# Projecting into transposed columns: which operand of the matmul stays, and which streams

## The chip, the cores and the metric

The kernel runs on one core of a Trainium2 chip. The metric is device time in microseconds (us) of one execution. The kernel before took 1302.33 us (median of three runs, 1302.3 to 1302.5).

## The reference

A sequence of 256 positions with 1024 features goes through two layers. Each layer is a half-step gated feed-forward network (FFN), a mixer, and a second half-step FFN; every part sits between a norm before and a norm after. The mixer of layer 0 is a dilated window attention with three groups of 16 heads, that of layer 1 a retention. Cut to what the change touches:

```
def rms_norm(x, g):
    y = xf * lax.rsqrt(jnp.mean(xf * xf, axis=-1, keepdims=True) + NORM_EPS)
    return y * g
def swiglu(h, w_gate, w_up, w_down):
    return (jax.nn.silu(h @ w_gate) * (h @ w_up)) @ w_down
...
    h = swiglu(rms_norm(x, g[0]), w_gate, w_up, w_down)      # 1024 -> 2816 -> 1024
    x = x + 0.5 * rms_norm(h, g[1])
    proj = (h @ w_in).reshape(B, S, 3 groups, q/k/v, 16 heads, 64)
    s = einsum('nbqhd,nbkhd->nbhqk', q, k) * 64 ** -0.5 + bias
...
```

Everything is float32. The projections of the norm before are linear, so the norm's gain can be folded into the weight's rows and its factor 1/rms, one number per position, can be applied behind the matmul.

## The kernel before, in words

**Positions** are held as two tiles of 128 (t = 0, 1). `xh` and `xl` hold the transposed input x of a part, features on the partitions, split into two float32r numbers whose sum is x; `pre_half` (L217) makes them with TensorE transposes.

**Weights** stream in once. `Stream` loads a block of 512 KB or 1 MB ("raw", two buffers), and `split` (L92) turns a piece of 256 rows by 512 columns (or 128 by 1024) into `whi` on ScalarE (L109, L115) and `wlo`, the rest, on VectorE (L110, L116). Six such pieces are in a ring, so splitting runs ahead of TensorE and is let on when TensorE gives a piece back (`done`, L135).

**A product** of x and w is three float32r matmuls, xh·whi, xh·wlo and xl·whi (`mm3`, L184 to L186). In all of them the x tile of 128 positions is the operand that stays in the array (LDWEIGHTS) and 512 weight columns stream. The result has positions on the partitions and columns along the row. A *unit* (`unit`, L319) is 512 output columns: 4 pieces of 2 row blocks, for 2 position tiles, 3 matmuls each, which is 48 matmuls of 512 columns into two PSUM banks.

**An FFN** (`ffn`, L363) has 11 units: gate and up columns in turn for five chunks of 512 (u = 0 to 9), and one unit of the last 256 gate and 256 up columns (u = 10). Behind a gate unit ScalarE takes Silu of the bank, scaled by the norm's factor `rstd` as one number per partition (L387); behind an up unit VectorE multiplies bank, factor and gate to h (L393). The down projection needs h with its columns on the partitions. So `h_store` (L336) transposes it, four blocks to a bank by TensorE (L342), ScalarE copies the bank to `hhf` (L349) and VectorE takes the rest `hlf` (L350). These transposes are put off to the second piece of the next unit (`pend`, `flush`). `down` (L414) then runs 22 row blocks and ends in `post` (L250): the norm behind the part, with its square sums, a small Newton iteration, and the sum with the residual.

**Attention** (`attn`, L532) has 18 units: q and k of three groups, then v of three groups, twice (8 heads each). q and k are wanted with the 64 numbers of a head on the partitions. After each q or k unit ScalarE copies the bank with the factor (L569), TensorE transposes eight blocks (L626), and VectorE copies them out (L628 for q, reversed; L630 for k).

**The order.** Each engine runs its instructions in one fixed order, which the language's scheduler makes from the program's order and from the buffers; inside `manual_schedule` it is the written one. Loads of weights and the small copies between layouts all go through SyncE's queue (SP). There are six PSUM banks for accumulators and two for transposes.

Of the kernel before, what the change touches and what calls it, by code (L numbers as in the profile page):

```python
# [14 lines left out]
P = 128  # L15
# [3 lines left out]
EPS = 1e-6  # L19
NK = D // P  # L20
# [120 lines left out]
class Trunk:  # L141
# [18 lines left out]
    def setup(self):  # L160
        nc, sb = self.nc, self.sb

        self.gcol = sb.tile([P, 96], F32, name="gcol")

        self.x = [sb.tile([P, D], F32, tag=f"x{t}", name=f"x{t}") for t in range(2)]
        xr = self.x_in[0].rearrange("(i r) d -> r i d", r=4)
        gr = sb.tile([96, P], F32, tag="sg", bufs=2, name="gr")
        nc.sync.dma_start(gr, self.norm_gains.rearrange("l n (k p) -> (l n k) p", p=P))
        for t in range(2):
            for rr in range(2):  # L170
                nc.sync.dma_start(self.x[t][rr * 64 : rr * 64 + 64, :], xr[2 * t + rr])
            self.ws.dma(halves=t == 0)
        self.ident = sb.tile([P, P], F32, name="ident")
        make_identity(nc, self.ident)
        warm = self.acc("warm")
# [29 lines left out]
    def rsqrt(self, ss, name, mean, out=None):  # L205

        nc, n = self.nc, ss.shape[1]
        t = self.sm.tile([P, 4 * n], F32, tag="nwt%d" % n, bufs=3, name=f"nw_{name}")
        v, y, u, r = (t[:, i * n : i * n + n] for i in range(4))
        nc.vector.tensor_scalar(out=v, in0=ss, scalar1=mean, scalar2=EPS, op0=ALU.mult, op1=ALU.add)  # L210
        self.newton(v, y, u)
        r = r if out is None else out
        nc.vector.tensor_scalar(out=r, in0=y, scalar1=1.0 / NEWTON, scalar2=None, op0=ALU.mult)
        return r


# [30 lines left out]
        self.pre_sums(name, 1, ss)  # L247
        self.rsqrt(ss, f"pre_{name}", 1.0 / D, self.rstd)

    def post(self, t, banks, gb, name):  # L250

        nc, sb = self.nc, self.sb
        w = self.sm.tile([P, 5], F32, tag="pn", bufs=3, name=f"pn_{name}_{t}")
        junk = sb.tile([P, 512], F32, tag="tmpb", bufs=1, name=f"psq_{name}_{t}")
        yg = sb.tile([P, D], F32, tag="tmpa", bufs=1, name=f"yg_{name}_{t}")
        for h in range(2):
            s = slice(h * 512, h * 512 + 512)
            nc.scalar.activation(junk, banks[h], AF.Square, scale=2.0**-5, accum_out=w[:, h : h + 1])
            nc.vector.tensor_tensor(out=yg[:, s], in0=banks[h], in1=gb[:, s], op=ALU.mult)
        v, y, u = (w[:, i : i + 1] for i in (2, 3, 4))  # L260
        nc.vector.scalar_tensor_tensor(out=v, in0=w[:, 0:1], scalar=EPS, in1=w[:, 1:2], op0=ALU.add, op1=ALU.add)
# [57 lines left out]
    def unit(self, pieces, accs, cols=(0, P), quota=2):  # L319
        for j, pc in enumerate(pieces):  # L320
# [3 lines left out]
                self.flush()  # L324
            self.work(quota)

    def flush(self):
        while self.pend:
            self.pend.pop(0)()
# [21 lines left out]

    def to_natural(self):

        self.xn = [self.sb.tile([P, D], F32, tag=f"E{t}", name=f"xn{t}") for t in range(2)]
        for T in range(2):
            for rr in range(2):
                for t in range(2):
                    self.nc.sync.dma_start(
                        self.xn[t].rearrange("(i r) d -> r i d", r=4)[2 * T + rr],
                        self.x[T][rr * 64 + 32 * t : rr * 64 + 32 * t + 32, :],  # L360
                    )

    def ffn(self, plan, nxt):  # L363
        nc, sb = self.nc, self.sb
        l, n = plan["l"], plan["n"]
        name = f"f{l}{n}"
        natural = l == 0 and n % 6 == 4
        for u, pieces in enumerate(plan["units"]):
            c = u // 2
            accs = {t: self.acc(f"ac_{name}_{u}_{t}") for t in range(2)}  # L370
            if u == 0:
                self.first_unit(pieces, accs)
                gb = self.load_gpost(l, n % 6 + 1, 0.5)
                self.hh = sb.tile([P, DFF // P, 2 * P], F32R, tag="A", name=f"hh{name}")
                self.hl = sb.tile([P, DFF // P, 2 * P], F32R, tag="B", name=f"hl{name}")
                if natural:
                    self.to_natural()
                if plan["tables"] is not None:
                    self.ret_tables(plan["tables"])
            else:  # L380
                self.unit(pieces, accs)
            w = 512 if u < 10 else 256
            if u % 2 == 0:
                sg = []
                for t in range(2):
                    g = sb.tile([P, 512], F32, tag="sg", bufs=2, name=f"sg_{name}{c}{t}")
                    nc.scalar.activation(g[:, :w], accs[t][:, :w], AF.Silu, scale=self.rstd[:, t : t + 1])  # L387
                    sg.append(g)
            if u % 2 == 1 or u == 10:
                for t in range(2):  # L390
                    h = sb.tile([P, 512], F32, tag="h", bufs=2, name=f"h_{name}{c}{t}")
                    up = accs[t][:, :512] if u < 10 else accs[t][:, 256:512]
                    nc.vector.scalar_tensor_tensor(out=h[:, :w], in0=up, scalar=self.rstd[:, t : t + 1], in1=sg[t][:, :w], op0=ALU.mult, op1=ALU.mult)  # L393
                    self.pend.append(lambda c=c, t=t, h=h, w=w: self.h_store(c, t, h, w, natural))
        hh, hl = self.hh, self.hl
        if natural:
            self.x = self.xn
        self.down(plan["down"], DFF // P, lambda k, t: (hh[:, k, t * P : (t + 1) * P], hl[:, k, t * P : (t + 1) * P]),
                  {3: self.flush}, gb, name, nxt)

    def first_unit(self, pieces, accs):

# [8 lines left out]

    TAIL = 5

    def down(self, pieces, rows, hT, hooks, gb, name, nxt, ntail=TAIL):  # L414


        ws = self.ws
        acc = [[self.acc(f"d_{name}_{t}{h}") for h in range(2)] for t in range(2)]
# [22 lines left out]
        self.post(0, acc[0], gb, name)  # L441
        for k in tail[:-2]:
            row(k, 1)
        for h in range(2):
# [5 lines left out]
                    self.pre_half(0, hh, name)  # L450
        if nxt is None:
            self.nc.sync.dma_start(self.out[0, :P, :], self.x[0])
            self.post(1, acc[1], gb, name)
# [5 lines left out]
        self.post(1, acc[1], gb, name)  # L459
        for h in range(2):  # L460
            self.pre_half(1, h, name)
        for k in tail[:2]:
# [69 lines left out]
    def attn(self, plan, nxt):  # L532
        nc, sb = self.nc, self.sb
        l = plan["l"]
        gb = self.load_gpost(l, 3, 1.0)
        OT = []
        rq = ru = None
        tasks_o1 = None
        for u, (o, kind, g, pieces) in enumerate(plan["units"]):
            accs = {t: self.acc(f"at_{u}_{t}") for t in range(2)}  # L540
            if kind == "q" and g == 0:
                bias, loads = self.bias_load(o)
            if u == 0:
                self.first_unit(pieces, accs)
                rq = self.sm.tile([P, 2], F32, tag="rq", name="rq")
# [3 lines left out]
                tr = self.trb("rut")  # L549
# [3 lines left out]
                nc.vector.tensor_copy(ru[0:64, :], tr[0:64, 0:2])  # L553
                nc.vector.tensor_copy(ru[64:128, 0:1], tr[64:128, 1:2])
                nc.vector.tensor_copy(ru[64:128, 1:2], tr[64:128, 0:1])
            else:
                for _ in range(2):
                    if loads:
                        loads.pop(0)()
                self.unit(pieces, accs, cols=(64, 192) if (kind == "v" and g == 2) else (0, P))  # L560
            if kind != "v":
                if kind == "q":
                    if g == 0:
                        qk = []
                    qk.append(sb.tile([P, 2, 4, 256], F32, tag=f"C{g}", name=f"qk{o}{g}"))
                w = 0 if kind == "q" else 1
                for t in range(2):
# [394 lines left out]
```

## Time and profile before

| | before |
|---|---|
| median of the runs | 1302.33 us |
| the profiled execution | 1302.6 us, its span 1300.5 us |
| TensorE (PE) matmuls busy | 1283.4 us, 99% of the span, 6326 records |
| TensorE weight loads (PEld) busy | 1052.9 us, 81% |
| VectorE (DVE) busy | 864.5 us, 66% |
| ScalarE (ACT) busy | 711.9 us, 55% |
| read from memory | 232.21 MB, 179 GB/s |
| granted TensorE clock, mean | 0.995 |

A row of the timeline gives the start of an instruction in us, its recorded length, engine, line, what it writes and reads, and shapes. Consecutive matmuls overlap in the records: each is listed at about 0.39 us, while the next one starts after little more than half of that. The time that a matmul costs is therefore read from start to start. In a row of the grouped view the number behind the bar is the group's busy time, then the mean recorded length in ns. An engine transpose and a float32 matmul (not float32r) are records of the same kind; the float32 matmul of the program stands as two records.

### The profile page before, as it was taken

Reading aid. Unit: us, or ns where it says so; the run is one execution under the profiler, and the core shown is the slowest. Engines: PE = TensorE matmul, PEld = TensorE weight load, DVE = VectorE, ACT = ScalarE, POOL = GpSimd, SP = SyncE. Lnnn points to the kernel's source line nnn. Section 1 sums busy time; section 2 is a strip of 40 time slices with the busy share of each in tenths; the row PEclk is TensorE's granted clock in tenths of the full one; section 3 lists DMA queues with packets and bytes.
Section 4 is the critical chain, followed back from the end, with each engine's and each line's share of the span. In section 5 each row is a group of like instructions: output and inputs, shape, how many; then the busy total and the mean of one; then the engine's idle time right before and its main releaser. Section 6 shows DMA issues by size and latency. Waiting matters only on the chain.

```text
span 1300.5 us, 16640 instructions
## 1 busy us (share of the span) xinstructions
PE 1283.4 (99%) x6326; PEld 1052.9 (81%) x6326; DVE 864.5 (66%) x1541; ACT 711.9 (55%) x1103; POOL 19.8 (2%) x16
## 2 busy tenths in 40 slices
PE   8999999999999999999999999999999999999997
PEld 6878887877887778888888888877888888888886
DVE  5765557678467768765477565489787775766544
ACT  4655444566555658764456554455555545565532
POOL 1000001000000000000000000000000000000000
PEclk8999999999999999999999999999999999999999
DMA  6755566754664346655547555645454555565551
GB/s 216 237 186 183 176 219 184 208 196 150 191 194 162 130 151 219 205 172 186 194 152 231 184 194 183 206 145 166 159 178 150 173 179 195 158 206 182 183 194 65
DMA packets 129692, 235.45 MB, mean 181 GB/s; under 512 B 25020, under 2 KB 41900, under 8 KB 129613
## 3 DMA queue, kind: packets, MB, share of 16 engines
q1 hardware_dynamic: 129468, 234.14, 55.6%
q8 instruction: 49, 0.80, 0.2%
q10 hardware_dynamic: 144, 0.26, 0.1%
q14 instruction: 31, 0.25, 0.1%
HBM read 232.21 MB, written 1.12 MB: 179 GB/s over the span
## 4 chain that ended last, share of the span: by engine, by line
PE 90%; DVE 4%; DMA 3%; ACT 2%; issue 1%; SPq 0%; DVEq 0%; ACTq 0%
PE ac_f L184 12%; PE ac_f L185 12%; PE ac_f L186 12%; PE d_f L184 6%; PE d_f L186 6%; PE d_f L185 6%; PE at L184 5%; PE at L186 5%; PE at L185 5%; PE rt L186 3%; PE rt L185 3%; PE rt L184 3%; DMA raw<-in_ret_w_in_dram 2%; PE htr L342 1%; DVE wlo L116 1%; PE ptt L678 1%
## 5 line engine op out<-in xcount | busy, mean ns | idle before, releaser
L116 DVE SCALAR_TENSOR_TENSOR wlo<-raw,gcol,whi 128x512 fp32r<-128x512 f32 x596 | 417.9, 749 | 184.3 <-ACT whi L115 183.5
L115 ACT ACTIVATE whi<-raw,gcol 128x512 fp32r<-128x512 f32 x596 | 393.7, 715 | 263.3 <-PE ac_f L186 88.4
L110 DVE TENSOR_TENSOR wlo<-raw,whi 128x1024 fp32r<-128x1024 f32 x112 | 137.3, 1226 | 137.9 <-ACT whi L109 137.6
L109 ACT ACTIVATE whi<-raw 128x1024 fp32r<-128x1024 f32 x112 | 118.8, 1061 | 165.3 <-PE d_f L186 101.2
L184 PE MATMUL d_f<-whi,hhf 128*128 128x512 f32 x352 | 137.6, 391 | 0.0
L186 PE MATMUL d_f<-whi,hlf 128*128 128x512 f32 x352 | 137.0, 389 | 0.0
L185 PE MATMUL d_f<-wlo,hhf 128*128 128x512 f32 x352 | 137.0, 389 | 0.0
L184 PE MATMUL at<-whi,xh_f 128*128 128x512 f32 x276 | 110.7, 401 | 0.0
L186 PE MATMUL at<-whi,xl_f 128*128 128x512 f32 x276 | 107.8, 391 | 0.0
L185 PE MATMUL at<-wlo,xh_f 128*128 128x512 f32 x276 | 107.4, 389 | 0.0
L185 PE MATMUL rt<-wlo,xh_f 128*128 128x512 f32 x244 | 95.8, 392 | 0.0
L184 PE MATMUL rt<-whi,xh_f 128*128 128x512 f32 x244 | 95.7, 392 | 0.0
L186 PE MATMUL rt<-whi,xl_f 128*128 128x512 f32 x244 | 95.1, 390 | 0.0
L186 PEld LDWEIGHTS d_f<-whi,hlf 128*128 128x128 f32 x352 | 66.1, 188 | 13.9
L184 PEld LDWEIGHTS d_f<-whi,hhf 128*128 128x128 f32 x352 | 66.1, 188 | 13.5
L185 PEld LDWEIGHTS d_f<-wlo,hhf 128*128 128x128 f32 x352 | 66.1, 188 | 13.4
L184 PE MATMUL ac_f<-whi,xh_in 128*128 128x512 f32 x176 | 70.4, 400 | 1.9 <-ACT whi L115 1.7
L185 PE MATMUL ac_f<-wlo,xh_in 128*128 128x512 f32 x176 | 69.9, 397 | 0.0
L186 PE MATMUL ac_f<-whi,xl_in 128*128 128x512 f32 x176 | 69.8, 396 | 0.0
L184 PE MATMUL ac_f<-whi,xh_at 128*128 128x512 f32 x168 | 65.9, 393 | 0.2 <-ACT xh_at L226 0.2
L186 PE MATMUL ac_f<-whi,xl_at 128*128 128x512 f32 x168 | 65.6, 390 | 0.0
L185 PE MATMUL ac_f<-wlo,xh_at 128*128 128x512 f32 x168 | 65.4, 389 | 0.0
(290 smaller groups left out, 2159.1 us busy)
## 6 DMA issues: line engine op xcount, KB each, us to landing
raw<-in_ffn_w_down_dram SPq DMA_DIRECT2D x44, 1024.0 KB, 4.9
raw<-in_ffn_w_up_dram SPq DMA_DIRECT2D x40, 1024.0 KB, 5.0
raw<-in_ffn_w_gate_dram SPq DMA_DIRECT2D x39, 1024.0 KB, 5.1
raw<-in_attn_w_in_dram SPq DMA_DIRECT2D x36, 1024.0 KB, 5.1
raw<-in_ret_w_in_dram SPq DMA_DIRECT2D x24, 1024.0 KB, 5.4
raw<-in_ret_w_in_dram SPq DMA_DIRECT2D x16, 512.0 KB, 4.6
raw<-in_ret_w_out_dram SPq DMA_DIRECT2D x8, 1024.0 KB, 4.9
raw<-in_ffn_w_gate_dram SPq DMA_DIRECT2D x10, 512.0 KB, 3.8
```

The lines of the kernel that those rows point to most:

```text
L109: nc.scalar.activation(hi, raw, AF.Copy)
L110: nc.vector.tensor_tensor(out=lo, in0=raw, in1=hi.bitcast(F32), op=ALU.subtract)
L115: nc.scalar.activation(hi[:, s], raw[:, s], AF.Copy, scale=gc)
L116: nc.vector.scalar_tensor_tensor(out=lo[:, s], in0=raw[:, s], scalar=gc, in1=hi[:, s].bitcast(F32), op0=ALU.mult, op1=ALU.subtract,)
L184: mm(out, xh, wh, start=start, stop=False)
L185: mm(out, xh, wl, start=False, stop=False)
L186: mm(out, xl, wh, start=False, stop=stop)
L342: nc.tensor.transpose(tr[:, k * P : (k + 1) * P], h[:, k * P : (k + 1) * P], self.ident)
L678: self.nc.tensor.transpose(tr[:, c * P : (c + 1) * P], pr[:, c * P : (c + 1) * P], self.ident)
```

## The change: what it does

For the FFN units u = 2 to 10 and for all q and k units but the first, the operands change places: 128 weight columns stay in the array and all 256 positions stream (`unit_t`). The result comes out with columns on the partitions, which is what the down projection and the scores want, so the transposes behind these units go. Each old matmul of 512 streamed columns becomes two of 256.

The norm's factor is then no longer one number per partition. `rows` makes it a row that is the same on all partitions (a diagonal matrix times ones, one float32 matmul), and VectorE multiplies the gate's bank, or the q or k bank, by it. The up half gets no factor in any unit: h stays too large by 1/rstd, one number per position, which the norm behind the part cancels, if its eps is multiplied by the variance of the norm before. `rsqrt` writes this scaled eps, `post` adds it in place of the constant, and where the positions are put into another order (`to_natural`) eight small copies move it too. The units u = 0 and 1 and the first q unit keep the old layout.

```
+    def unit_t(self, pieces, accs, quota=2):
+        mm = self.nc.tensor.matmul
+        for j, pc in enumerate(pieces):
+            hi, lo = self.ws.get(pc)
+            for kk in range(2):
+                k = 2 * j + kk
+                xh, xl = (z[:, k, 0 : 2 * P] for z in (self.xh, self.xl))
+                for c in range(4):
+                    b, a = divmod(c, 2)
+                    out = accs[b][:, a * 256 : a * 256 + 256]
+                    s = slice(kk * 512 + c * P, kk * 512 + c * P + P)
+                    mm(out, hi[:, s], xh, start=k == 0 and a == 0, stop=False, ...)
+                    mm(out, hi[:, s], xl, start=False, stop=False, ...)
+                    mm(out, lo[:, s], xh, start=False, stop=k == NK - 1, ...)
+            self.ws.done(pc)
+            if j == 1:
+                self.flush()
+            self.work(quota)
+    def ffn_t(self, u, pieces, name, natural, st):
+        accs = [self.acc(f"ac_{name}_{u}_{b}") for b in range(2)]
+        self.unit_t(pieces, accs)
+        if u % 2 == 0:
+            r = st["r"].unsqueeze(1).to_broadcast([P, 2, 2 * P])
+            for b in range(2 if u < 10 else 1):
+                g = sb.tile([P, 512], F32, tag="sg", bufs=2, ...)
+                nc.vector.tensor_tensor(out=g..., in0=accs[b]..., in1=r, op=ALU.mult)
+                nc.scalar.activation(g, g, AF.Silu)
...
+        for b, up in enumerate(accs if u < 10 else accs[1:]):
+            nc.vector.tensor_tensor(out=h, in0=up, in1=st["sg"][b], op=ALU.mult)
...
+            nc.scalar.activation(hi, hv, AF.Copy)
+            nc.vector.tensor_tensor(out=lo, in0=hv, in1=hi.bitcast(F32), op=ALU.subtract)
+    def rows(self, cols, name):
+        for t in range(2):
+            nc.vector.tensor_scalar(out=d[:, t, :], in0=self.ident, scalar1=cols[:, t : t + 1], ...)
+        nc.tensor.matmul(tr[:, : 2 * P], self.ones, d, start=True, stop=True)
+        nc.vector.tensor_copy(r, tr[:, : 2 * P])
 in rsqrt:
+            nc.vector.tensor_scalar(out=self.eps, in0=v, scalar1=EPS, scalar2=None, op0=ALU.mult)
 in post:
-        nc.vector.scalar_tensor_tensor(out=v, in0=w[:, 0:1], scalar=EPS, in1=w[:, 1:2], ...)
+        nc.vector.scalar_tensor_tensor(out=v, in0=w[:, 0:1], scalar=EPS if eps is None else eps[:, t : t + 1], in1=w[:, 1:2], ...)
 in to_natural, eight times:
+                    self.nc.sync.dma_start(self.eps[:, t : t + 1]...[2 * T + rr], eps[rr * 64 + 32 * t : rr * 64 + 32 * t + 32, T : T + 1])
 in ffn:
+            if u > 1:
+                self.ffn_t(u, pieces, name, natural, st)
+                continue
...
+                self.pend.append(lambda: st.update(r=self.rows(self.rstd, "f")))
...
-                    nc.vector.scalar_tensor_tensor(out=h[:, :w], in0=up, scalar=self.rstd[:, t : t + 1], in1=sg[t][:, :w], ...)
+                    nc.vector.tensor_tensor(out=h, in0=accs[t], in1=sg[t], op=ALU.mult)
 in attn:
+                self.pend.append(lambda rq=rq: scales.update(q=self.rows(rq, "q"), k=self.rows(self.rstd, "k")))
...
+                if kind == "v":
+                    self.unit(...)
+                else:
+                    self.unit_t(pieces, accs)
...
+                if u:
+                    for b in range(2):
+                        dst = qk[g][:, w, 2 * b : 2 * b + 2, :].rearrange("p a (r i) -> p a r i", r=4)
...
+                        nc.vector.tensor_tensor(out=dst, in0=src, in1=sc..., op=ALU.mult)
```

How the instructions stand before and after is shown at three places. The first is TensorE in unit 4 of the first FFN, at the end of its second piece; `ac_f_4_0` and `ac_f_4_1` are the unit's two banks, `htr` a bank for transposes. Before:

```order
L186 MATMUL ac_f_4_1_547<-whi_452,xl_in 128x512
L342 MATMUL htr_591<-ident,h_f_542 128x128 x4
L342 MATMUL htr_598<-ident,h_f_544 128x128 x4
L184 MATMUL ac_f_4_0_546<-whi_478,xh_in 128x512
L185 MATMUL ac_f_4_0_546<-wlo_479,xh_in 128x512
L186 MATMUL ac_f_4_0_546<-whi_478,xl_in 128x512
```

After:

```order
L377 MATMUL ac_f_4_1_660<-xh_in,wlo_512 128x256
L375 MATMUL ac_f_4_0_659<-xh_in,whi_551 128x256
L376 MATMUL ac_f_4_0_659<-xl_in,whi_551 128x256
L377 MATMUL ac_f_4_0_659<-xh_in,wlo_552 128x256
L375 MATMUL ac_f_4_1_660<-xh_in,whi_551 128x256
```

The eight transposes are gone, and every matmul streams 256 instead of 512. In the whole program 2256 instructions on L184 to L186 have become 4512 on L375 to L377.

The second place is VectorE behind the gate unit 2 and the up unit 3 of the first FFN (`sg` is the gate, `hlf` the rest of h). Before:

```order
L116 SCALAR_TENSOR_TENSOR wlo_497<-raw_406,gcol,whi_496 128x512 x2
L393 SCALAR_TENSOR_TENSOR h_f_542<-ac_f_3_0_464,rstd_in,sg_f_460 128x512
L116 SCALAR_TENSOR_TENSOR wlo_517<-raw_458,gcol,whi_516 128x512 x2
L393 SCALAR_TENSOR_TENSOR h_f_544<-ac_f_3_1_465,rstd_in,sg_f_462 128x512
L350 TENSOR_TENSOR hlf_277<-htr_591,hhf_276 128x4x128
```

After:

```order
L344 TENSOR_TENSOR sg_f_519<-ac_f_2_0_379,rowsf 128x512
L344 TENSOR_TENSOR sg_f_522<-ac_f_2_1_380,rowsf 128x512
L116 SCALAR_TENSOR_TENSOR wlo_482<-raw_373,gcol,whi_481 128x512 x2
L351 TENSOR_TENSOR h_f_651<-ac_f_3_0_525,sg_f_519 128x512
L351 TENSOR_TENSOR h_f_655<-ac_f_3_1_526,sg_f_522 128x512
L360 TENSOR_TENSOR hlf_281<-h_f_651,hhf_280 128x512
```

VectorE now also has the gate's two multiplications, ahead of ScalarE's Silu, and `hlf` reads h itself and no longer a bank of transposes.

The third place is TensorE in unit 1 of attention, where `rows` makes the two rows of factors (`rw_q`, `rw_k`) among the transposes `qkt` of the first q unit. After:

```order
L390 MATMUL rw_q<-dg_q,ones 128x256
L375 MATMUL at_0_2177<-xh_f_1988,whi_2078 128x256
L390 MATMUL rw_k<-dg_k,ones 128x256
L716 MATMUL qkt_2257<-ident,nat_2173 128x128 x4
L376 MATMUL at_0_2177<-xl_f_1989,whi_2078 128x256
L716 MATMUL qkt_2263<-ident,nat_2175 128x128 x4
```

Four users share the two transpose banks there, where before only the two `qkt` did. The rows in between that repeat the unit's matmuls are left out.

More of the change, by code (lines that the diff above doesn't have):

```diff
@@ L213, in rsqrt @@
         nc.vector.tensor_scalar(out=r, in0=y, scalar1=1.0 / NEWTON, scalar2=None, op0=ALU.mult)
+        if out is not None:
+            self.eps = self.sm.tile([P, n], F32, tag="eps", bufs=2, name=f"eps_{name}")
+            nc.vector.tensor_scalar(out=self.eps, in0=v, scalar1=EPS, scalar2=None, op0=ALU.mult)
         return r
@@ L248, in pre_stats, with post @@
         self.rsqrt(ss, f"pre_{name}", 1.0 / D, self.rstd)
-    def post(self, t, banks, gb, name):
+    def post(self, t, banks, gb, name, eps=None):
         nc, sb = self.nc, self.sb
@@ L260, in post @@
         v, y, u = (w[:, i : i + 1] for i in (2, 3, 4))
-        nc.vector.scalar_tensor_tensor(out=v, in0=w[:, 0:1], scalar=EPS, in1=w[:, 1:2], op0=ALU.add, op1=ALU.add)
+        nc.vector.scalar_tensor_tensor(out=v, in0=w[:, 0:1], scalar=EPS if eps is None else eps[:, t : t + 1], in1=w[:, 1:2], op0=ALU.add, op1=ALU.add)
         self.newton(v, y, u)
@@ new lines, in unit_t @@
+    def unit_t(self, pieces, accs, quota=2):
[9 more added lines that the diff above has]
+                    s = slice(kk * 512 + c * P, kk * 512 + c * P + P)
+                    mm(out, hi[:, s], xh, start=k == 0 and a == 0, stop=False, skip_group_check=True)
+                    mm(out, hi[:, s], xl, start=False, stop=False, skip_group_check=True)
+                    mm(out, lo[:, s], xh, start=False, stop=k == NK - 1, skip_group_check=True)
+            self.ws.done(pc)
+            if j == 1:
+                self.flush()
+            self.work(quota)
@@ new lines, in rows @@
+    def rows(self, cols, name):
+        nc, sb = self.nc, self.sb
+        d = sb.tile([P, 2, P], F32, tag="dg", name=f"dg_{name}")
+        for t in range(2):
+            nc.vector.tensor_scalar(out=d[:, t, :], in0=self.ident, scalar1=cols[:, t : t + 1], scalar2=None, op0=ALU.mult)
+        tr = self.trb(f"rw_{name}")
+        nc.tensor.matmul(tr[:, : 2 * P], self.ones, d, start=True, stop=True)
+        r = sb.tile([P, 2 * P], F32, tag=f"rows{name}", name=f"rows{name}")
+        nc.vector.tensor_copy(r, tr[:, : 2 * P])
+        return r
@@ L352, in to_natural @@
     def to_natural(self):
+        eps, self.eps = self.eps, self.sm.tile([P, 2], F32, tag="eps", bufs=2, name="epsn")
         self.xn = [self.sb.tile([P, D], F32, tag=f"E{t}", name=f"xn{t}") for t in range(2)]
@@ L361, in to_natural @@
                     )
+                    self.nc.sync.dma_start(
+                        self.eps[:, t : t + 1].rearrange("(i r) d -> r i d", r=4)[2 * T + rr],
+                        eps[rr * 64 + 32 * t : rr * 64 + 32 * t + 32, T : T + 1],
+                    )
     def ffn(self, plan, nxt):
@@ L398, in ffn @@
         self.down(plan["down"], DFF // P, lambda k, t: (hh[:, k, t * P : (t + 1) * P], hl[:, k, t * P : (t + 1) * P]),
-                  {3: self.flush}, gb, name, nxt)
+                  {3: self.flush}, gb, name, nxt, eps=eps)
     def first_unit(self, pieces, accs):
@@ L412, with down @@
     TAIL = 5
-    def down(self, pieces, rows, hT, hooks, gb, name, nxt, ntail=TAIL):
+    def down(self, pieces, rows, hT, hooks, gb, name, nxt, ntail=TAIL, eps=None):
         ws = self.ws
@@ L440, in down @@
         order.__enter__()
-        self.post(0, acc[0], gb, name)
+        self.post(0, acc[0], gb, name, eps)
         for k in tail[:-2]:
@@ L452, in down @@
             self.nc.sync.dma_start(self.out[0, :P, :], self.x[0])
-            self.post(1, acc[1], gb, name)
+            self.post(1, acc[1], gb, name, eps)
             for h in range(2):
@@ L458, in down @@
             return
-        self.post(1, acc[1], gb, name)
+        self.post(1, acc[1], gb, name, eps)
         for h in range(2):
@@ L537, in attn @@
         rq = ru = None
+        scales = {}
         tasks_o1 = None
@@ L559, in attn @@
                         loads.pop(0)()
-                self.unit(pieces, accs, cols=(64, 192) if (kind == "v" and g == 2) else (0, P))
+                if kind == "v":
+                    self.unit(pieces, accs, cols=(64, 192) if g == 2 else (0, P))
+                else:
+                    self.unit_t(pieces, accs)
             if kind != "v":
```

36 lines of the change are left out of this document (28 added, 8 removed).

## The prediction

> **What bounds the kernel now.** I read the page first: busy times and the chain that ended last.
>
> ```profile
> PE 1283.4 (99%) x6326; PEld 1052.9 (81%) x6326; DVE 864.5 (66%) x1541; ACT 711.9 (55%) x1103; POOL 19.8 (2%) x16
> PE 90%; DVE 4%; DMA 3%; ACT 2%; issue 1%; SPq 0%; DVEq 0%; ACTq 0%
> ```
>
> TensorE holds 90% of the chain and is busy in 99% of the span, while the engines that feed it have a third of the time or more to spare. So the change is priced on TensorE's own queue, and the others only if they get late. Busy is no price, since records overlap; starts are. The timeline of TensorE where the second FFN passes from its last unit to the down projection shows both kinds of work:
>
> ```profile
> 599.68 0.39 PE L184 MATMUL ac_f<-whi,xh_at 128*128 128x512 f32 x1
> ...
> 611.01 0.39 PE L186 MATMUL d_f<-whi,hlf 128*128 128x512 f32 x1
> 611.25 0.60 PE L342 MATMUL htr<-ident,h_f 128*128 128x128 f32 x4
> 611.60 0.48 PE L184 MATMUL d_f<-whi,hhf 128*128 128x512 f32 x1
> 611.91 0.40 PE L185 MATMUL d_f<-wlo,hhf 128*128 128x512 f32 x1
> ```
>
> From 599.68 to 611.01 stand 50 starts: **226.6 ns for a matmul of 512 streamed columns**. From 611.01 to 611.91, 0.90 us, two of these spacings (0.453) are the matmuls' own; four transposes cost 0.447 us. A group of eight, in attention:
>
> ```profile
> 221.20 0.39 PE L186 MATMUL at<-whi,xl_f 128*128 128x512 f32 x1
> 221.44 1.03 PE L626 MATMUL qkt<-ident,nat 128*128 128x128 f32 x8
> 222.22 0.48 PE L184 MATMUL at<-whi,xh_f 128*128 128x512 f32 x1
> 222.54 0.40 PE L185 MATMUL at<-wlo,xh_f 128*128 128x512 f32 x1
> ```
>
> 1.34 us less 0.453 is 0.887 us for eight.
>
> **What goes.** The grouped rows count the transposes:
>
> ```profile
> L342 PE MATMUL htr<-ident,h_f 128*128 128x128 f32 x176 | 23.1, 272 | 0.0
> L626 PE MATMUL qkt<-ident,nat 128*128 128x128 f32 x96 | 12.4, 272 | 0.0
> ```
>
> Eight stay in each of four FFNs (chunk 0) and eight in attention, so 144 and 88 go: 27 groups of eight and, behind u = 10, four groups of four. 27 × 0.887 + 4 × 0.447 = **25.7 us less**.
>
> **What is recut.** 9 units in 4 FFNs and 11 in attention, 47 units of 48 matmuls: 2256 × 226.6 ns = 511.2 us. They become 4512 of 256 columns, each with its own weight load. What one of these, p, costs decides the case: the sum breaks even near p = 118 (below). The trace of before has no float32r matmul of 256 columns, so p is bounded.
>
> *From below*, by the weight load. It overlaps the matmul before it, and the two must take turns. After a pause in attention:
>
> ```profile
> 286.35 0.19 PEld L184 LDWEIGHTS at<-whi,xh_f 128*128 128x128 f32 x1
> 286.46 0.19 PEld L185 LDWEIGHTS at<-wlo,xh_f 128*128 128x128 f32 x1
> 286.69 0.19 PEld L186 LDWEIGHTS at<-whi,xl_f 128*128 128x128 f32 x1
> ```
>
> The first load meets an empty array; the next one starts 0.11 us later, when the first has made room, and the third 0.23 later, one matmul on. So a load occupies its place for 0.11 us, although its record says 0.19. The groups of transposes agree, eight of them at 0.11 each. p is not below 110 ns.
>
> *From above*, by what a matmul has beside its columns. At the start the clock is halved (the last two rows are of the view by stretches: length, then busy time of TensorE, weight loads, VectorE, ScalarE and GpSimd, granted clock, DMA share, GB/s):
>
> ```profile
> 10.65 0.63 PE L184 MATMUL ac_f<-whi,xh_in 128*128 128x512 f32 x1
> ...
> 14.06 0.63 PE L186 MATMUL ac_f<-whi,xl_in 128*128 128x512 f32 x1
> 10.50:14.00 3.50, 3.50 (x9) 2.67 (x9) 1.42 (x2) 1.24 (x2) 0.00 (x0) 0.50 1.04 336
> 600.00:604.00 4.00, 4.00 (x20) 3.30 (x19) 2.93 (x4) 2.20 (x3) 0.00 (x0) 1.00 0.85 262
> ```
>
> Eight spacings in 3.41 us at a granted clock of 0.50 are 426 ns, half of which is 213. At a clock of 1.00 it is 226.6. So 13.5 ns of the spacing do not come from the array's clock. If they are paid once per matmul, p is 106.6 + 13.5 = **120**; if they are paid per column (operands delivered more slowly than the array could take them at full clock), p is half of 226.6, **113.3**. At half the clock a fixed extra should show too, and nothing is left over there; a delivery rate would hide. I take the reading per column, and 1 ns for a part that is paid once: **p = 114.5**, 4512 × 114.5 = 516.6, **5.4 us more**.
>
> A rule of the Trainium skill stands between these readings: "TensorE: Matmul & The Clock Gate", section "Back-to-back issue gap", gives a full-clock spacing of the columns over 2.4 GHz plus some 2.5 ns, which would be 109 ns here, an estimate by that page. For 512 columns it gives 216, where this trace has 226.6, so the trace does not agree, and the forecast does not use it.
>
> **What is added to TensorE.** Six float32 matmuls of 256 columns (`rows`: one in each FFN, two in attention), each two records. The nearest row:
>
> ```profile
> L848 PE MATMUL rs<-rc 128*128 128x256 f32 x32 | 8.0, 392 | 0.7 <-ACT rc L839 0.7
> ```
>
> 8.0 us over 32 records, 0.25 each: 12 × 0.25 = **3.0 us more**. In the FFNs the diagonal is ready half a unit before its matmul. In attention two rows and two banks of transposes share two PSUM banks inside one piece: the second `qkt` waits until VectorE has copied `rw_k` out. Behind TensorE's wait stand the unit's matmuls. From one copy of 256 columns (below 0.69 us, the row of 512 below) to nothing; I take **0.6 us**.
>
> **The other engines.** The rows of the work that is exchanged:
>
> ```profile
> L116 DVE SCALAR_TENSOR_TENSOR wlo<-raw,gcol,whi 128x512 fp32r<-128x512 f32 x596 | 417.9, 749 | 184.3 <-ACT whi L115 183.5
> L350 DVE TENSOR_TENSOR hlf<-htr,hhf 128x512 fp32r<-128x512 f32 x40 | 29.5, 780 | 0.6 <-ACT hhf L349 0.5
> L259 DVE TENSOR_TENSOR yg_f<-d_f,gpost 128x512 f32<-128x512 f32 x16 | 11.0, 689 | 15.2 <-ACT psq_f L258 15.2
> L393 DVE SCALAR_TENSOR_TENSOR h_f<-ac_f,rstd_in,sg_f 128x512 f32<-128x512 f32 x10 | 7.2, 744 | 0.0
> L630 DVE COPY qk<-qkt 128x512 f32<-128x512 f32 x12 | 8.0, 686 | 6.4 <-PE qkt L626 6.4
> 680.00:810.00 130.00, 130.00 (x597) 108.07 (x596) 79.72 (x109) 71.67 (x107) 0.00 (x0) 1.00 0.59 194
> ```
>
> A chunk's pair of units had on VectorE 16 splits (749), two products (744), two rests (780): 15.0 us. Now it has 16 splits and six operations at 689, the row of a plain two-operand product out of PSUM: 16.1 us of about 22. VectorE goes from 79.72 in 130 us, 61%, to about 66%. In attention one product replaces one copy (686), and ScalarE loses 22 copies. The cover is the ring of six pieces, 2.7 us of TensorE each: the row of L116 shows 184.3 us in which VectorE waited with nothing to do. VectorE's new wait for the end of a gate unit holds back the splits queued behind it by at most the two products, 1.4 us, against a lead of two pieces or more. I count nothing. Were that cover gone, it would be 1.4 us in the 16 gate units u = 2 to 8 and half of it in the four of u = 10, 25 us.
>
> The scaled eps is an instruction on two columns per norm, and `post` reads a number per partition where it read a constant: nothing. The eight small copies stand in SP's queue among weight loads, behind the rstd of the second FFN. That queue then holds back the next load:
>
> ```profile
> 488.13 0.37 SPq L79 DMA_DIRECT2D raw<-in_ffn_w_gate_dram  x1
> 488.55 0.52 SPq L358 DMA_DIRECT2D xn<-x  x1
> 493.23 0.37 SPq L79 DMA_DIRECT2D raw<-in_ffn_w_gate_dram  x1
> ```
>
> At 0.5 us per issue they take 4 us of a queue that had 4 us between two loads there, and what is late then is a raw block two pieces ahead of the split: nothing, at worst 4 us once.
>
> **The sum.** −25.7 + 5.4 + 3.0 + 0.6 = −16.7 us. The profiled execution took 1302.6 us (span 1300.5), the median is 1302.33, so both give 1286: **1285.7 us** predicted. Break-even: (511.2 + 25.7 − 3.6) / 4512 = 118.2 ns.
>
> **The rivals.**
>
> *The extra is paid once per matmul.* p = 120, for the place is every one of the 4512 matmuls: 541.4 us, 30.2 more, 1302.3 − 22.1 + 30.2 = **1310**, slower; the kernel is slower from p = 118.2 on. For it: 13.5 ns look like a start, and each matmul changes weights. Against it: the half clock shows none of it. To p = 122.5 it reaches 1322. Chance 0.30.
>
> *The weight load sets the pace,* the columns themselves running at the array's clock, 106.6, below the load's 110. 496.3 us, 14.9 less: 1302.3 − 22.1 − 14.9 = **1265**. For it: the spacing of loads above. Against it: a 512 matmul has twice the time of its load and still takes 226.6, so its columns are not at the array's clock. Chance 0.12. The Trainium skill's 109 would land here, 4 us lower, an estimate by that page.
>
> *Loads are not hidden any more.*
>
> ```profile
> L184 PEld LDWEIGHTS at<-whi,xh_f 128*128 128x128 f32 x276 | 51.8, 188 | 10.1
> L626 PEld LDWEIGHTS qkt<-ident,nat 128*128 128x128 f32 x96 | 11.2, 140 | 1.6
> ```
>
> With the recorded 188 ns of a load as its cost p = 188, 848 us, 1302.3 − 22.1 + 337 = **1617**. Against it: transposes, whose loads are recorded at 140, follow each other every 110. Chance 0.03. The Trainium skill, "Perfetto Trace Analysis", section "Identifying the Most-Contended Engine", asks for the busy share of weight loads as the measure of TensorE; it is 81% here, and by the records' length it would pass 100%, which speaks against the change. This trace bears out only that records overlap.
>
> *The feeding engines get late,* VectorE's products before each Silu in front of the splits: the 25 us above, 1285.7 + 25 = **1311**. Against it: the 184.3 us of idle time and TensorE's 130.00 busy of 130. Chance 0.06.
>
> **How the numbers follow.** The forecast, p from 112.5 to 117, gives 1277 to 1297 with a chance of 0.49; the four rivals take 0.30, 0.12, 0.03 and 0.06. A measurement tells 0.2%, 2.6 us, from no change: faster is p below 117.6, slower above 118.8. Faster holds the forecast, the weight load's pace and a little of the first rival: 0.63. Within 0.2%: 0.06, the first rival's lower edge. Slower: the rest, 0.31. The range for 8 in 10 leaves out part of the weight load's pace below and the high part of the slow cases above: 1267 to 1314. The forecast's own is 1277 to 1297.
>
> **What would show it.** In the changed kernel's timeline the starts of the matmuls on L375 to L377: 113 to 116 ns is this forecast, 120 the first rival, 110 the second. Loads with idle time between them mean that columns set the pace, loads end to end that they do. The transposes should number 40 instead of 272, at the six `rows` TensorE should lose about 3.6 us in all, and in the FFN windows TensorE should stay busy all the time. The prediction is wrong if the spacing is over 118, or if TensorE idles behind gate units.

## The result: slower by 0.6%

The changed kernel takes 1310.38 us (median of six runs, 1309.44 to 1311.59), the kernel before 1302.58 beside it (six runs). The ratio is 1.0059, 95% interval 1.0046 to 1.0072: **7.7 us slower** (6.0 to 9.4), where 16.7 us less were forecast. The first rival gave 1310.

| | before | after |
|---|---|---|
| profiled execution, span | 1302.6, 1300.5 us | 1309.4, 1307.6 us |
| TensorE not busy (span less busy) | 17.1 us | 18.3 us |
| products into `ac_f` and `at` (FFN and attention units), start to next start | 690.6 us | 721.4 us |
| transposes `htr` and `qkt`, the same | 27.1 us | 3.9 us |
| `rows`, the same | – | 1.8 us |

The last three rows are sums over the trace from each matmul's start to the next start on TensorE; a pause counts for the matmul ahead of it, and what a group of transposes costs the matmul behind it counts with the products. They make 717.7 us before and 727.1 after, 9.3 more, so the loss lies in the products. The two spans differ by 7.1 us; most of the rest is in the down projections, whose products take 1.8 us less in the profile after (a pause of the profile before is in it, shown below).

### The profile after

The page of the changed kernel, busy times and the chain that ended last:

```profile
PE 1289.3 (99%) x8362; PEld 1148.9 (88%) x8362; DVE 893.0 (68%) x1593; ACT 695.9 (53%) x1073; POOL 19.8 (2%) x17
PE 90%; DVE 4%; DMA 2%; ACT 2%; issue 1%; SPq 0%; DVEq 0%; ACTq 0%
```

TensorE still holds 90% of the chain, so no other engine has become the bound. What one of the new matmuls costs stands in TensorE's timeline in the second FFN, start and recorded length first:

```profile
599.83 0.28 PE L377 MATMUL ac_f<-xh_at,wlo 128*128 128x256 f32 x1
...
603.91 0.28 PE L375 MATMUL ac_f<-xh_at,whi 128*128 128x256 f32 x1
```

34 spacings in 4.08 us: **p = 120.0 ns**. The forecast needed 114.5, and the kernel is slower from 118.2 on. The groups of like instructions, with count, busy us and mean ns, show that the rest was done as the code says:

```profile
L410 PE MATMUL htr<-ident,h_f 128*128 128x128 f32 x32 | 4.1, 272 | 0.0
L716 PE MATMUL qkt<-ident,nat 128*128 128x128 f32 x8 | 1.2, 276 | 0.1
L390 PE MATMUL rw_f<-dg_f,ones 128*128 128x256 f32 x8 | 2.4, 387 | 1.8 <-DVE dg_f L388 1.8
L344 DVE TENSOR_TENSOR sg_f<-ac_f,rowsf 128x512 f32<-128x512 f32 x36 | 24.5, 691 | 1.4 <-PE ac_f L377 0.4
L351 DVE TENSOR_TENSOR h_f<-ac_f,sg_f 128x512 f32<-128x512 f32 x36 | 24.6, 689 | 0.9
```

40 transposes are left, and the two new products cost VectorE what the forecast gave them (689). The view by stretches of the third FFN (length; busy time of TensorE, weight loads, VectorE, ScalarE, GpSimd; clock; DMA share; GB/s):

```profile
680.00:810.00 130.00, 130.00 (x986) 125.59 (x985) 86.62 (x131) 69.98 (x104) 0.00 (x0) 1.00 0.60 195
```

VectorE has 86.62 of 130 us, 67%, against 61% before, and TensorE has no idle time in this stretch: nothing waits behind a gate unit there. One pause is new. TensorE and then VectorE in the first FFN, when the row of factors is made (in brackets the idle time ahead and what ended it):

```profile
30.09 0.40 PE L187 MATMUL ac_f<-wlo,xh_in 128*128 128x512 f32 x1
32.26 0.67 PE L390 MATMUL rw_f<-dg_f,ones 128*128 128x256 f32 x2 [1.77 <-DVE dg_f L388]
27.77 0.28 DVE L388 TENSOR_SCALAR dg_f<-ident,rstd_in 128x128 f32<-128x128 f32 x1
29.17 2.74 DVE L116 SCALAR_TENSOR_TENSOR wlo<-raw,gcol,whi 128x512 fp32r<-128x512 f32 x4 [1.12 <-ACT whi L115]
31.83 0.28 DVE L388 TENSOR_SCALAR dg_f<-ident,rstd_in 128x128 f32<-128x128 f32 x1
```

VectorE makes the first half of the diagonal, then four splits, which wait for ScalarE, and only then the second half. TensorE stands for about 2 us. `rw_f` in the other three FFNs shows no idle time ahead of it, as the 1.8 us of the group's row are this one pause.

### The profile page after: what moved, and what is told of

It reads as the page before. It is cut to its first block, busy times and chain, and to the rows that moved or that the text cites. A ratio compares the mean times of both kernels' runs of the same rounds, so it can differ in the third digit from the quotient of the medians.

```text
span 1307.6 us, 20776 instructions
## 1 busy us (share of the span) xinstructions
PE 1289.3 (99%) x8362; PEld 1148.9 (88%) x8362; DVE 893.0 (68%) x1593; ACT 695.9 (53%) x1073; POOL 19.8 (2%) x17
## 4 chain that ended last, share of the span: by engine, by line
PE 90%; DVE 4%; DMA 2%; ACT 2%; issue 1%; SPq 0%; DVEq 0%; ACTq 0%
PE ac_f L375 11%; PE ac_f L377 11%; PE ac_f L376 11%; PE d_f L187 6%; PE d_f L186 6%; PE d_f L188 6%; PE rt L188 4%; PE rt L187 4%; PE rt L186 4%; PE at L376 3%; PE at L377 3%; PE at L375 3%; PE at L186 2%; PE at L188 2%; PE at L187 2%; PE ac_f L186 1%
## 5 line engine op out<-in xcount | busy, mean ns | idle before, releaser
L186 PE MATMUL d_f<-whi,hhf 128*128 128x512 f32 x352 | 137.2, 390 | 0.0
L376 PE MATMUL at<-xl_f,whi 128*128 128x256 f32 x352 | 99.7, 283 | 0.0
L375 PE MATMUL at<-xh_f,whi 128*128 128x256 f32 x352 | 99.7, 284 | 0.0
L377 PE MATMUL at<-xh_f,wlo 128*128 128x256 f32 x352 | 99.6, 283 | 0.0
L186 PE MATMUL rt<-whi,xh_f 128*128 128x512 f32 x244 | 95.6, 392 | 0.2 <-ACT xh_f L232 0.2
L375 PE MATMUL ac_f<-xh_in,whi 128*128 128x256 f32 x288 | 81.8, 284 | 0.0
L376 PE MATMUL ac_f<-xl_in,whi 128*128 128x256 f32 x288 | 81.6, 283 | 0.0
L377 PE MATMUL ac_f<-xh_in,wlo 128*128 128x256 f32 x288 | 81.6, 283 | 0.0
L375 PE MATMUL ac_f<-xh_at,whi 128*128 128x256 f32 x288 | 81.6, 283 | 0.0
L375 PE MATMUL ac_f<-xh_rt,whi 128*128 128x256 f32 x288 | 81.6, 283 | 0.0
L375 PE MATMUL ac_f<-xh_f,whi 128*128 128x256 f32 x288 | 81.6, 283 | 0.0
L377 PE MATMUL ac_f<-xh_at,wlo 128*128 128x256 f32 x288 | 81.5, 283 | 0.0
L377 PE MATMUL ac_f<-xh_rt,wlo 128*128 128x256 f32 x288 | 81.5, 283 | 0.0
```

The source lines that it names most:

```text
L186: mm(out, xh, wh, start=start, stop=False)
L375: mm(out, hi[:, s], xh, start=k == 0 and a == 0, stop=False, skip_group_check=True)
L376: mm(out, hi[:, s], xl, start=False, stop=False, skip_group_check=True)
L377: mm(out, lo[:, s], xh, start=False, stop=k == NK - 1, skip_group_check=True)
```

## The experiments

The forecast had stood on one open number, the 13.5 ns that a matmul of 512 takes beyond its columns at the array's clock. Two theories of it were left. *Fixed part* (F in the expectations): each matmul pays it once, so the spacing is the columns' own time (213.1 ns for 512, half of the 426.2 at the halved clock, and in proportion for fewer) and some 13.4, and no less than a load's turn of 110. *Per column* (W): the spacing is in proportion to columns down to some floor that a load sets, and the 120 of the new matmuls is that floor. A third possibility is that it isn't the cut at all, but the exchange of operands (X).

### Matmul widths by themselves

The kernel before, with series of 24 equal matmuls put into unit 3 of the first FFN, their results unused:

```
+            if self.probe and u == 3:
+                W, X = self.ws.get(pieces[0])[0], self.xh[:, 0, 0:P]
+                for _ in range(24):
+                    mm(pr[:, :512], X, W[:, :512], start=True, stop=True)
+                ... the same with 448, 384, 320, 256, 192, 128, 64 columns
+                ... with X[:, :64] and X[:, :32] as weights, and in bfloat16
```

> The kernel before with rows of extra matmuls put ahead of unit 3 of the first FFN (24 of each kind, their result is used by nobody), and 14 more at the very start, while the clock is still halved. Theory F (each float32r matmul pays 13.3 ns once at full clock): float32r spacing with 128 weight columns is columns / 2.4 + 13.3 ns: 226.6 at 512, 200 at 448, 173 at 384, 147 at 320, 120 at 256; below that the weight load takes over at about 110 (192, 128 and 64 columns). With 64 or 32 weight columns, a shorter load, 256 stay at 120 and 128 fall to 67. Theory W (the weight load sets the pace at 256, load 107 plus 13 to hand over, and the 13.5 ns at 512 are paid per column): 198 at 448, 170 at 384, 142 at 320, 120 at 256, 192, 128 and 64; with 64 weight columns 113 at 256. If the 13.3 ns belong to float32r alone, bfloat16 has about 216 at 512 and 109 or less at 256; if every matmul pays them, 227 and 120. At the start 213 at 256 columns if the halved clock hides the extra.

TensorE's timeline; a row gathers a series, its length runs from the first start to the last end:

```profile
51.36 5.60 PE L390 MATMUL probe<-whi,xh_in 128*128 128x512 f32 x24
56.80 5.03 PE L392 MATMUL probe<-whi,xh_in 128*128 128x448 f32 x24
61.67 4.35 PE L394 MATMUL probe<-whi,xh_in 128*128 128x384 f32 x24
65.86 3.67 PE L396 MATMUL probe<-whi,xh_in 128*128 128x320 f32 x24
69.37 3.04 PE L398 MATMUL probe<-whi,xh_in 128*128 128x256 f32 x24
72.24 2.82 PE L400 MATMUL probe<-whi,xh_in 128*128 128x192 f32 x24
74.90 2.81 PE L402 MATMUL probe<-whi,xh_in 128*128 128x128 f32 x24
80.20 7.29 PE L406 MATMUL probe<-whi,xh_in 128*64 128x512 f32 x24
87.33 2.89 PE L408 MATMUL probe<-whi,xh_in 128*64 128x256 f32 x24
90.06 1.60 PE L410 MATMUL probe<-whi,xh_in 128*64 128x128 f32 x24
91.50 2.99 PE L412 MATMUL probe<-whi,xh_in 128*32 128x256 f32 x24
94.56 5.13 PE L414 MATMUL probe<-zb 128*128 128x512 bf16 x23
99.52 2.78 PE L416 MATMUL probe<-zb 128*128 128x256 bf16 x24
```

Length less one recorded matmul, over the number of spacings, is the spacing. The recorded lengths are in the groups, two of them here:

```profile
L390 PE MATMUL probe<-whi,xh_in 128*128 128x512 f32 x24 | 5.6, 389 | 0.0
L398 PE MATMUL probe<-whi,xh_in 128*128 128x256 f32 x24 | 3.0, 283 | 0.0
```

So 512 columns give (5.60 − 0.389) / 23 = 226.6 ns, and 256 give (3.04 − 0.283) / 23 = 119.9. In the same way, to some 0.3 ns, since the rows give hundredths of a us:

| columns | 512 | 448 | 384 | 320 | 256 | 192 | 128 |
|---|---|---|---|---|---|---|---|
| measured, ns | 226.6 | 202.8 | 174.6 | 146.1 | 119.9 | 110.7 | 110.3 |
| 213.1 × columns / 512 | 213.1 | 186.5 | 159.8 | 133.2 | 106.6 | 80 | 53 |
| beyond that | 13.5 | 16.3 | 14.8 | 12.9 | 13.3 | load's turn | load's turn |
| per column would give | 226.6 | 198.3 | 170.0 | 141.6 | 113.3 | | |

The extra does not shrink with the columns: it is paid once per matmul. At 192 and 128 columns the load's turn of 110 ns sets the pace. The per-column reading, on which the forecast stood, is refuted, and so is a floor of 120, since narrower matmuls go at 110.

What the extra is stays open. With 64 weight columns 256 take 113.6 ns (7.0 extra) and 128 take 59.9 (6.6), where F had expected 120 and 67 and W 113 for 256; so the floor of 110 goes with the load of 128 columns, and the extra isn't the same for every load. But 32 weight columns give 117.8 at 256, and 512 columns on 64 weights go two ways. The view by stretches and the timeline of two parts of that series:

```profile
81.00:84.00 3.00, 3.00 (x9) 1.57 (x8) 0.00 (x0) 0.00 (x0) 0.00 (x0) 0.52 0.00 0
80.86 3.41 PE L406 MATMUL probe<-whi,xh_in 128*64 128x512 f32 x8
84.11 3.39 PE L406 MATMUL probe<-whi,xh_in 128*64 128x512 f32 x14
```

From 81 to 84 us the granted clock is 0.52, and the starts are 427 ns apart (3.41 less the last record of 0.42, over 7): no extra, as at the start of the kernel before. Behind it, at a clock of 1.00, the spacing is 230.7 ns (3.39 less 0.39, over 13), 17.6 extra, more than with 128 weight columns. No rule by weight columns fits all of these. With bfloat16 the spacings are 216.0 and 109.0, 2.9 and 2.4 extra, so the large extra belongs to float32r; whether to its load or to its streaming this doesn't tell, since both operands changed their type and the trace has no records of the loads of these series.

A series at the very start of the kernel, meant for the halved clock, can't be read: 256 columns follow each other there every 213 ns, which would be half the clock without an extra, but the view by stretches gives a clock of 1.00.

The Trainium skill, "TensorE: Matmul & The Clock Gate", section "Back-to-back issue gap", gives columns over 2.4 GHz plus some 2.5 ns at full clock. The bfloat16 rows agree with it; the float32r rows, with 13 ns, don't.

### The cut alone, in the old layout

The kernel before, with each of the 2256 matmuls that the change recuts made into two of 256 columns, the operands left in their places and the transposes kept:

```
+                for a in range(2):
+                    s = slice(kk * 512 + a * 256, kk * 512 + a * 256 + 256)
+                    out = accs[t][:, a * 256 : a * 256 + 256]
+                    mm(out, xh, hi[:, s], ...)
+                    mm(out, xh, lo[:, s], ...)
+                    mm(out, xl, hi[:, s], ...)
...
-                self.unit(pieces, accs)
+                self.unit(pieces, accs, half=u > 1)
```

> The kernel before, layout and transposes as they were, only that in the 47 units of the change each matmul of 512 weight columns is cut into two of 256. Theory F, and W too: 4512 matmuls at 120 instead of 2256 at 226.6, 30 us more: 1332 to 1334 us, spacing 120. Rival X (the 120 come from which operand stays in the array and which streams, not from the width): spacing 113, 1302 to 1304 us.

Measured: 1329.18 us against 1301.49, ratio 1.0208 (1.0192 to 1.0224), **27.1 us more** (25.0 to 29.2). TensorE's timeline, 35 spacings:

```profile
599.75 0.28 PE L329 MATMUL ac_f<-whi,xh_at 128*128 128x256 f32 x1
...
603.95 0.28 PE L331 MATMUL ac_f<-whi,xl_at 128*128 128x256 f32 x1
```

120.0 ns again, with x in the array and weights streaming. So it is the cut that costs, and which operand stays makes no difference. The cost is some 3 us below the 30.2 that 47 units of 48 × (240 − 226.6) ns give. Summed from start to start, the products into `ac_f` and `at` go from 690.6 to 719.0 us, 28.4 more: the matmuls that are recut take 229.0 on average in the kernel before and their halves 120.8, not the 226.6 and 120.0 of undisturbed stretches.

### The change in attention alone

The old FFNs and the old eps, with the 11 q and k units of attention in the new layout; against the changed kernel:

```
                 else:
                     self.unit_t(pieces, accs)
 ...
-            if u > 1:
-                self.ffn_t(u, pieces, name, natural, st)
-                continue
```

> The change in the 11 q and k units of attention alone, FFNs as before. By F a unit loses 48 x (2 x 120 - 226.6) = 0.64 us and wins 0.89 us of transposes: 11 x -0.25 = -2.7, two row matmuls and their waits +1.0 to 1.6: -1 to -2 us, 1301 to 1301.5. Rival (the loss sits in waits for rows and buffers in attention, not in the matmuls): 1304 or more.

Measured: 1297.64 us, ratio 0.9968 (0.9955 to 0.9981), **4.2 us less** (2.5 to 5.9). The sign is the expected one, the size more than expected. By price a unit here pays 0.64 us for the cut and wins a whole group of eight transposes, 0.887. From start to start attention's matmuls, transposes and rows go from 212.4 us to 210.6, 1.8 less, as the price said. The other 2 us or so lie elsewhere. The profile of before has a pause of 1.28 us at the end of a down projection, where that of attention alone has 0.46 and the others have 0.26 to 0.87:

```profile
848.81 0.39 PE L186 MATMUL d_f<-whi,hlf 128*128 128x512 f32 x1
850.47 0.63 PE L222 MATMUL xtr_f<-ident,xn 128*128 128x128 f32 x4 [1.28 <-DVE xn L265]
```

That is one profile, and whether the timed runs of the kernel before have it can't be read. This rest is not settled.

### The change in the FFNs alone

The reverse: the new FFNs and scaled eps, with the attention of before; against the changed kernel:

```
-                if kind == "v":
-                    self.unit(...)
-                else:
-                    self.unit_t(pieces, accs)
+                self.unit(...)
```

> The change in the FFNs alone, attention as before. By F 36 units lose 0.64 us each, 23.0; 20 groups of transposes win 16.0; four row matmuls cost 2, and the wait of 2.2 us that the changed kernel's trace shows ahead of the first of them stays: +9 to +11 us, 1311.5 to 1313.5. Rival (the loss sits in attention): below 1306.

Measured: 1311.04 us, ratio 1.0071 (1.0058 to 1.0084), **9.2 us more** (7.5 to 10.9). The price by rows gives the same: 36 units × 0.64 = 23.2 for the cut, less 16.0 for 16 groups of eight and 4 of four transposes, and 2.0 for four `rows` at 0.5. That it agrees to the digit is luck: the sum leaves out the pause ahead of the first `rw_f`, 1.76 us of idle time in this profile too, and prices the cut a little too high, as the run above showed. In an FFN transposes stood behind every second unit only, so two cuts, 1.29 us, are paid for 0.887. The two parts make 9.2 − 4.2 = 5.0, the whole measured 7.7; the intervals overlap.

### The pause in the first FFN

The changed kernel, with the FFN's row of factors asked for behind unit 1, one unit later:

```
 behind unit 0:
-                self.pend.append(lambda: st.update(r=self.rows(self.rstd, "f")))
 behind unit 1:
+                self.pend.append(lambda: st.update(r=self.rows(self.rstd, "f")))
```

> The changed kernel, with the FFNs' row of factors asked for behind unit 1 instead of behind unit 0, so that its diagonal is ready long before TensorE comes to it. If the pause of 2.2 us ahead of the first row matmul (the second diagonal instruction stands on VectorE behind four splits that wait for ScalarE) is lost time of the whole, -2 us against the changed kernel: 1307 to 1308.5. If TensorE catches it up because the splits run late there anyway, no change: 1309.5 or more.

Measured: 1311.27 us against 1301.16, ratio 1.0082 (1.0067 to 1.0097). Nothing is won. TensorE and VectorE in this kernel:

```profile
45.55 0.28 PE L375 MATMUL ac_f<-xh_in,whi 128*128 128x256 f32 x1
47.14 0.65 PE L410 MATMUL htr<-ident,h_f 128*128 128x128 f32 x4 [1.31 <-DVE rowsf L392]
44.01 2.74 DVE L116 SCALAR_TENSOR_TENSOR wlo<-raw,gcol,whi 128x512 fp32r<-128x512 f32 x4 [1.57 <-ACT whi L115]
46.67 0.42 DVE L392 COPY rowsf<-rw_f 128x256 f32<-128x256 f32 x1
```

The pause before `rw_f` is gone, and one of 1.3 us of idle time stands at the transposes of chunk 0 that come with it now: they want a bank that VectorE copies out only behind four splits. It is the same wait behind the same queue, one place on. So the pause is real, but this experiment doesn't show what the kernel would take without it.

### One load for two products

If the extra goes with the load or start, one load of `whi` that serves xh and xl side by side, 512 columns, should take it away from one matmul in three. First for the time alone; this kernel leaves out the adding of the two halves and the banks of their own that they would need, so its sums land in wrong places:

```
-                    mm(out, hi[:, s], xh, ...)
-                    mm(out, hi[:, s], xl, ...)
+                    two = accs[b].rearrange("p (z c) -> p z c", z=2)
+                    mm(two, hi[:, s], self.xx[:, k, :, 0 : 2 * P], ...)
                     mm(out, lo[:, s], xh, ...)
```

> The changed kernel with xh and xl side by side in one tile, so that one load of whi serves 512 streamed columns (xh and xl) and 1504 loads of 4512 go: 1504 matmuls of 512 and 1504 of 256. It leaves out that the two halves would have to be added and have banks of their own: the sums land in wrong places, so its time is only that of the matmuls. If the extra belongs to the weight load (13.3 ns each at 128 float32r columns): 1504 x (226.6 + 120.0) = 521.3 us instead of 4512 x 120.2 = 542.3, -21 us against the changed kernel, about 1289. If it belongs to streamed columns or to the end of each output region: no change, about 1310.

Measured: 1294.13 us against 1301.16, ratio 0.9944 (0.9926 to 0.9962); its span is 1292.3, **15.3 below the changed kernel's**. TensorE's timeline, five pairs in 1.74 us:

```profile
599.28 0.40 PE L376 MATMUL ac_f<-xx_at,whi 128*128 128x512 f32 x1
599.51 0.28 PE L377 MATMUL ac_f<-xx_at,wlo 128*128 128x256 f32 x1
...
601.02 0.39 PE L186 MATMUL d_f<-whi,hhf 128*128 128x512 f32 x1
```

A pair costs 348 ns where three of 256 cost 360. Summed over the trace, the 1504 triples go from 543.6 to 527.8 us, 15.8 less and 10.5 ns each, instead of the 13.3 of a whole fixed part. So a load and start saved gives most of the extra back, less than the 21 us that were expected in all. That is the second proof of a cost per matmul, by taking it away.

### The stacked form complete, in attention and everywhere

Here the two halves of a bank are added: ScalarE copies one half out, VectorE adds the other, then the multiplications follow as before. A unit takes two of its weight blocks at a time through all four pieces, then the other two.

```
+        for z in range(2):
+            accs = [self.acc(f"{name}_{z}_{b}") for b in range(2)]
             for j, pc in enumerate(pieces):
...
+                        mm(two, hi[:, s], self.xx[:, k, :, 0 : 2 * P], ...)
+                        mm(accs[b][:, 0 : 2 * P], lo[:, s], self.xh[:, k, 0 : 2 * P], ...)
...
+                self.nc.scalar.activation(lo2[...], accs[b][:, 256:512], AF.Copy)
+                self.nc.vector.tensor_tensor(out=sm[...], in0=accs[b][:, 0:256], in1=lo2[...], op=ALU.add)
+            evac(z, sm)
```

First with the old FFNs, stacked in attention's 11 units:

> As attn_only, and there one load of whi serves 512 streamed columns (xh and xl side by side); two weight blocks at a time go over all pieces, so that each has a bank of its own, whose two halves are added when it is emptied (ScalarE copies one, VectorE adds). By the cost per load and the spacing of the run with the sums in wrong places, 32 blocks a unit at 351 ns instead of 361: 11 x 0.31 = -3.4 us against attn_only, about 1294 (0.994 of before). If the additions, or the pieces that are now held for half a unit longer, make TensorE wait, no gain against attn_only: 1297 or more.

Measured: 1295.78 us against 1302.69, ratio 0.9946 (0.9933 to 0.9960). By the ratios that is 2.9 us below attention alone in the unstacked form, where 3.4 were expected, and the two intervals just overlap. From start to start the products into `at` fell from 209.2 to 206.2 us.

Then in all 47 units of the changed kernel:

> The changed kernel with the same in all 47 units, the additions included. If ScalarE and VectorE keep up, the time of the run with the sums in wrong places: 1293 to 1296. VectorE has then 19.6 us of work in a pair of FFN units of 22 us instead of 16.1, and pieces are held longer; if that makes TensorE wait, more: 1300 to 1320.

Measured: **1293.79 us** against 1302.69, ratio 0.9936 (0.9924 to 0.9949), 8.3 us less than before. It beats both kernels. Its page, the stretch in the third FFN and TensorE's timeline in the second:

```profile
PE 1274.6 (99%) x6858; PEld 1066.6 (82%) x6858; DVE 956.1 (74%) x1781; ACT 752.9 (58%) x1265; POOL 19.8 (2%) x17
680.00:810.00 130.00, 130.00 (x714) 112.39 (x713) 98.73 (x153) 81.30 (x141) 0.00 (x0) 1.00 0.58 199
599.68 0.40 PE L375 MATMUL ac_f<-xx_at,whi 128*128 128x512 f32 x1
...
602.15 0.40 PE L187 MATMUL d_f<-whi,hhf 128*128 128x512 f32 x1
```

Seven pairs take 2.47 us, 353 ns each. VectorE has 98.73 of 130 us, 76%, and TensorE still no idle time in this stretch. The transposes saved are now more than the cut costs. Against the stacked attention alone the FFNs add little: the two intervals overlap.

## Why the prediction was wrong

**The step that failed** is the reading of the 13.5 ns "per column", hence p = 114.5. The runs put 120.0 there, and the cut alone costs 27.1 us, not 5.4. That is 21.7 of the 24.4 us between forecast and result.

**What misled** was the halved clock: "a fixed extra should show too, and nothing is left over there". The spacing of 213 × 2 at the halved clock is a fact of the trace, and the 427 ns in the series on 64 weights bear it out, but the conclusion from it isn't: the series by width show a fixed extra at full clock all the same. Why the halved clock hides it stays open; a wait that runs beside the columns and fits into their longer time would do so, but no run tests that. The argument on the other side, "13.5 ns look like a start, and each matmul changes weights", led to the right price and was given 0.30; whether the change of weights is the reason stays open.

**The rivals.** "The extra is paid once per matmul" gave 1310 and is what happened, by its own mechanism. That it hit the microsecond is luck: it took 30.2 us for the cut, which alone cost 27.1, and 22.1 for what is won, where the runs give 19.4 (below). "The weight load sets the pace" fell: 110 is the floor, but 256 columns take 120 and stand above it. "Loads are not hidden" fell with it. The busy share of weight loads went from 81% to 88%, and TensorE's stayed at 99%: since records overlap, neither share tells by how much a matmul got dearer, the starts do. For the same reason the test by idle time between loads, which the prediction named, tells nothing: 985 loads are recorded as 125.59 of 130 us, though the turn of one is 110 ns. The rule of the Trainium skill ("Perfetto Trace Analysis", "Identifying the Most-Contended Engine") that judges TensorE by the loads' busy share, beside its share of peak arithmetic, pointed to the right side here, but not by its reason: the loads' turn of 110 ns did not set the pace. "The feeding engines get late" fell, but for the one pause in the first FFN: 130.00 of 130 in the third.

**What held.** The transposes fell to 40. Transposes less `rows` and waits were to win 25.7 − 3.6 = 22.1 us; the runs give 27.1 − 7.7 = 19.4. The two intervals allow the difference; the pause in the first FFN, which the forecast counted as nothing, may be the greater part of it, but no run shows that. VectorE was forecast at 66% of the FFN stretch and has 67%. In attention the waits around the rows are small. TensorE there, from the last matmul ahead of `rw_k` to the first in step behind it:

```profile
227.66 0.28 PE L375 MATMUL at<-xh_f,whi 128*128 128x256 f32 x1
227.78 0.66 PE L390 MATMUL rw_k<-dg_k,ones 128*128 128x256 f32 x2
...
229.63 0.28 PE L375 MATMUL at<-xh_f,whi 128*128 128x256 f32 x1
```

1.97 us hold three matmuls (0.36), `rw_k` (0.5) and eight transposes (0.887), which leaves 0.2 us of waiting where 0.6 was taken.

**What else was wrong.** "In the FFNs the diagonal is ready half a unit before its matmul" holds in three of four FFNs; in the first, four splits stand between its halves. The eight copies of eps were counted as nothing, and TensorE's time not busy grew by 1.2 us in all, with that pause in it, so they can't have cost it much. SP's queue there, start and time:

```profile
490.01 0.37 SPq L79 DMA_DIRECT2D raw<-in_ffn_w_gate_dram  x1
492.50 1.74 SPq L431 DMA_DIRECT2D epsn<-eps_pre_at  x3
495.19 0.37 SPq L79 DMA_DIRECT2D raw<-in_ffn_w_gate_dram  x1
```

Three copies take 1.74 us, 0.58 each against the 0.5 assumed, and the two weight loads are 5.2 us apart where they were 5.1.

## What to carry to other kernels

Before a matmul is cut into narrower ones, measure the spacing at the new width in a short series: a price per matmul that hides in a long stream, 13 of 227 ns, doubles when the stream is halved, and here that was more than all the transposes saved. Price a change of layout unit by unit, for the same exchange gained where each unit got rid of eight transposes and lost where two units shared them. Where several products share their stationary operand, let one load serve a stream that holds them side by side, even if another engine then has to add the halves.

## What the runs showed of the hardware that was not expected

- A float32r matmul with 128 weight columns takes 13 to 16 ns beyond its columns at full clock, from 256 columns to 512 (119.9 and 226.6); bfloat16 takes 2 to 3 (109.0 and 216.0). With 64 weight columns it is 7 at 128 and 256 columns, and 17.6 at 512.
- At 192 columns and at 128 the spacing stays at 110 ns, the turn of a load of 128 float32r columns, although such a load is recorded at 188 to 192.
- At the halved clock the extra of a 512 matmul isn't there: 426 ns a spacing with 128 weight columns, 427 with 64. No run explains it.
- One load that serves 512 columns instead of two that serve 256 each saves 10.5 ns on average of a triple's 361.
